# An elementwise add and GELU on one core: the first two loads of y cut 2 + 6 MB instead of 4 + 4, in one buffer, and the last wait moved from VectorE to ScalarE

## The chip, the cores and the metric

The kernel runs on one core of a Trainium2 chip. The time is that of one execution on the device, in microseconds (us). The profile shows one execution in detail; its times count from the first instruction's start. In it DVE is VectorE, ACT is ScalarE, POOL is GpSimd and SP is SyncE, the engine that issues all transfers here. TensorE computes nothing in this kernel, and the granted clock is 1.000 throughout.

## The reference

Two float32 arrays of 1024 x 4096 go in and one of the same shape comes out, 16.78 MB each:

```python
z = x + y
return (0.5 * z * (1 + np.tanh(np.sqrt(2 / np.pi) * (z + 0.044715 * z ** 3)))).astype(np.float32)
```

The kernel computes it as max(z, 0) + g(-|z|), where g is the tanh form of GELU. The two agree, since g(z) - g(-z) = z.

## The kernel before, in words

Each of the 128 partitions holds eight rows of the arrays, so 32768 columns in a row of 128 KB. The columns are worked in 16 chunks of 2048 (`CH`). A chunk c takes four steps:

- `add(c)`, L149: z = x + y, in place in the buffer that x was loaded into. VectorE does chunks 0, 2, 4, 6, 8 and 12, GpSimd the ten others.
- `mag(c)`, L154, and `gelu(c)`, L157: ScalarE takes |z| into a PSUM buffer and then the GELU of minus that, in place. There are two PSUM buffers (`PS = 2`), so `mag(c)` waits until `end(c - 2)` has read the buffer.
- `end(c)`, L166: VectorE forms max(z, 0) + w, in place in z. For chunk 8 (`FIRST`) it comes in two halves.

In the texts below add2 is `add(2)`, and so on. The whole of z, 128 KB in a partition, stays on the chip. y passes through two buffers of 8192 columns.

SP issues all nine transfers, in one queue, in this order: y0, x0, y1, x1, y2, y3, store 0, store 1, store 2 (L173, L174). The loads of x have 16384 columns each (8 MB), those of y 8192 (4 MB), the stores 16384, 10240 and 6144 (8, 5 and 3 MB). `begin_early` moves the first two ahead of the barrier at the start. y2 goes into the buffer of y0 and so waits on SP for add0 to add3; y3 waits for add4 to add7. Store 0 waits for end0 to end7 and, by a dependence that is put in by hand (L138), for the first half of end8. Store 1 waits for end12, store 2 for end15.

The order on each engine is written out by hand. GpSimd does its adds in rising order. ScalarE does mag0, gelu0, mag1, gelu1 and so on. VectorE's order comes from `by_dve`, which says ahead of which end each of its adds stands:

```python
    by_dve = {0: 0, 2: 0, 4: 2, 6: 4, 8: 8, 12: 10}
```

That gives add0, add2, end0, end1, add4, end2, end3, add6, end4, end5, end6, end7, add8, end8 (two halves), end9, add12, end10 to end15. An engine works its list in order, so an instruction that waits holds up those behind it.

At the end, `wait_late` takes the wait for the last store's landing out of SP's wait for everything. It is put at the very end of the program, as a wait of one engine that also sets the semaphore back.

Of the kernel before, what the change touches and what calls it, by code (L numbers as in the profile page):

```python
# [8 lines left out]
def begin_early(nc, count):  # L9


    head, body = (b.instructions for b in nc.main_func.blocks[:2])
    SP = mybir.EngineType.SP
    moved = [i for i in body if i.engine == SP and isinstance(i, mybir.InstDMACopy)][:count]
    assert not any(i.sync_info and i.sync_info.on_wait for i in moved)
    assert all(i.regs_accessed() == ((), ()) for i in moved)
    at = next(k for k, i in enumerate(head) if i.engine == SP)
    for k, i in enumerate(moved):
        body.remove(i)
        head.insert(at + k, i)  # L20


def wait_late(nc):

    body, end = (b.instructions for b in nc.main_func.blocks[1:3])
    last = [i for i in body if isinstance(i, mybir.InstDMACopy)][-1]
    (sem,) = [u.id for u in last.sync_info.on_update]
    all_done = end[0]  # L30
    reset = next(i for i in end if isinstance(i, mybir.InstDrain) and i.is_reset_sema)
    at = end.index(reset)
    clear = end[at + 1]
    first, stop = reset.reset_range_start, reset.reset_range_stop
    assert all_done.engine == mybir.EngineType.SP and reset.engine == mybir.EngineType.Pool
    assert isinstance(clear, mybir.InstISA) and clear.engine == mybir.EngineType.Pool
    waits = all_done.sync_info.on_wait
    (its,) = [w for w in waits if w.id == sem]

    end[0] = mybir.InstDrain(  # L40
        name=all_done.name, engine=all_done.engine, debug=all_done.debug, is_reset_sema=False,
        sync_info=mybir.SyncInfo(on_wait=[w for w in waits if w.id != sem], on_update=[]),
    )
    parts = []
    for f, e in ((first, sem), (sem + 1, stop)):
        if f < e:
            nc.gpsimd.sem_clear(range(f, e))
            parts.append(nc.cur_bb.bb.instructions.pop())
    end[at + 1 : at + 2] = parts
    end.append(  # L50
        mybir.InstEventSemaphore(
            name=clear.name, engine=mybir.EngineType.DVE, debug=clear.debug,
            sync_info=mybir.SyncInfo(
                on_wait=[its],
                on_update=[
                    mybir.SyncUpdate(
                        sync_type="semaphore", id=sem, ant_name=its.ant_name,
                        update_mode="sem-sub-imm", update_value=its.wait_value,
                    )
                ],  # L60
            ),
        )
    )


@with_exitstack
def kernel(
    ctx: ExitStack,
    tc: tile.TileContext,
    x: bass.AP,  # L70
    y: bass.AP,
    out: bass.AP,
):

    nc = tc.nc
    P = nc.NUM_PARTITIONS
    fp32 = mybir.dt.float32
    act = mybir.ActivationFunctionType
    alu = mybir.AluOpType

    N, D = x.shape
    assert N % P == 0
    TOT = N // P * D  # L90
    xv, yv, ov = (a.rearrange("(p n) d -> p (n d)", p=P) for a in (x, y, out))

    YS = 8192
    CH = 2048
    PS = 2
    xloads = [16384, 16384]
    yloads = [8192, 8192, 8192, 8192]
    FIRST = 8
    stores = [16384, 10240, 6144]

    def ranges(sizes):
        ends = [sum(sizes[: i + 1]) for i in range(len(sizes))]
        assert ends[-1] == TOT
        return [(e - f, e) for e, f in zip(ends, sizes)]

    xr, yr, sr, cr = (ranges(r) for r in (xloads, yloads, stores, [CH] * (TOT // CH)))
    C = len(cr)

    by_dve = {0: 0, 2: 0, 4: 2, 6: 4, 8: 8, 12: 10}

    def over(rs, lo, hi):
        return [i for i, (a, b) in enumerate(rs) if a < hi and b > lo]

    pool_sb = ctx.enter_context(tc.tile_pool(name="xz", bufs=1))
    pool_y = ctx.enter_context(tc.tile_pool(name="y", bufs=2))
    pool_w = ctx.enter_context(
        tc.tile_pool(name="w", bufs=PS, space=bass.MemoryType.PSUM)
    )

    zt = pool_sb.tile([P, TOT], fp32, tag="z", name="z")  # L120
    yt, wt, ends = {}, {}, {}

    def load_x(i):
        a, b = xr[i]
        nc.sync.dma_start(out=zt[:, a:b], in_=xv[:, a:b])

    def load_y(i):
        a, b = yr[i]
        s, o = divmod(a, YS)
        if o == 0:  # L130
            yt[s] = pool_y.tile([P, YS], fp32, tag="y", name=f"y{s}")
        nc.sync.dma_start(out=yt[s][:, o : o + b - a], in_=yv[:, a:b])  # L132

    def store(i):
        a, b = sr[i]
        ins = nc.sync.dma_start(out=ov[:, a:b], in_=zt[:, a:b])
        if i == 0:
            tc.add_manual_dep(  # L138
                ins.ins,
                ends[FIRST].name,  # L140
                mybir.DependencyInfo(mybir.DependencyClass.Sync, mybir.DependencyReason.DATA),
                reason="the stores join the queue when the last load is nearly done",
            )

    def add(c):
        a, b = cr[c]
        s, o = divmod(a, YS)
        eng = nc.vector if c in by_dve else nc.gpsimd
        eng.tensor_add(out=zt[:, a:b], in0=zt[:, a:b], in1=yt[s][:, o : o + b - a])  # L149

    def mag(c):
        a, b = cr[c]
        wt[c] = pool_w.tile([P, CH], fp32, tag="w", name=f"w{c}")
        nc.scalar.activation(out=wt[c], in_=zt[:, a:b], func=act.Abs)  # L154

    def gelu(c):
        nc.scalar.activation(  # L157
            out=wt[c], in_=wt[c], func=act.Gelu_apprx_tanh, scale=-1.0
        )

    def end(c):
        a, b = cr[c]
        parts = 2 if c == FIRST else 1
        n = (b - a) // parts
        for o in range(0, b - a, n):
            ins = nc.vector.scalar_tensor_tensor(  # L166
                out=zt[:, a + o : a + o + n], in0=zt[:, a + o : a + o + n], scalar=0.0,
                in1=wt[c][:, o : o + n], op0=alu.max, op1=alu.add,
            )
            ends.setdefault(c, ins.ins)  # L170


    sp = [(load_y, 0), (load_x, 0), (load_y, 1), (load_x, 1), (load_y, 2), (load_y, 3)]  # L173
    sp += [(store, i) for i in range(len(stores))]  # L174
    pool = [(add, c) for c in range(C) if c not in by_dve]
    dve, acts = [], []
    for c in range(C):
        dve += [(add, k) for k in sorted(by_dve) if by_dve[k] == c] + [(end, c)]
        acts += [(mag, c), (gelu, c)]

    needs = {
        load_x: lambda i: [],
        load_y: lambda i: [
            (add, c) for c in over(cr, yr[i][0] - 2 * YS, yr[i][1] - 2 * YS)
        ],
        add: lambda c: [(load_x, i) for i in over(xr, *cr[c])]
        + [(load_y, i) for i in over(yr, *cr[c])],
        mag: lambda c: [(add, c)] + ([(end, c - PS)] if c >= PS else []),
        gelu: lambda c: [(mag, c)],
        end: lambda c: [(gelu, c)],  # L190
        store: lambda i: [(end, c) for c in over(cr, *sr[i])] + [(end, FIRST)],
    }
    queues = [sp, pool, acts, dve]
    done = set()
    with tc.manual_schedule():
        one = pool_sb.tile([P, 1], fp32, tag="one", name="one")
        nc.vector.memset(one, 0.0)  # L197
        nc.scalar.activation(out=one, in_=one, func=act.Gelu_apprx_tanh)  # L198
        while any(queues):
            moved = False  # L200
            for q in queues:
                while q and all(n in done for n in needs[q[0][0]](q[0][1])):
                    fn, arg = q.pop(0)
                    fn(arg)
                    done.add((fn, arg))
                    moved = True
                    if q is not sp:
                        break
            assert moved, [q[:1] for q in queues]

    ctx.close()
    tc.close()
    tc.compile()  # L213
    begin_early(nc, 2)
    wait_late(nc)


# [28 lines left out]
```

## Time and profile before

| what | us |
|---|---|
| median of 3 runs | 120.11 (120.06 to 120.14) |
| the profiled execution | 120.11 |
| its span | 118.7 |
| VectorE busy, 24 instructions | 59.8 |
| ScalarE busy, 34 instructions | 60.8 |
| GpSimd busy, 14 instructions | 55.5 |
| one add on GpSimd, x10, mean | 5.56 |
| one add on VectorE, x6, mean | 4.01 |
| one mag and one gelu on ScalarE, x16, mean | 1.88 and 1.86 |
| one end on VectorE, x17, mean | 2.16 |

The table has the busy times of the page and the means of its groups by line. A mean mixes cases: an add of VectorE took between 2.28 and 6.59, one of GpSimd between 4.50 and 6.63. The nine transfers moved 50.33 MB in 1296 packets, at 424 GB/s over the span. In the slices each digit is the busy share of a fortieth of the span (2.97 us) in tenths. In lines of the timeline the first number is the start, the second the time, and the bracket tells how long the engine had been idle and what released it. The time of a transfer from issue to landing is in lines of its own, as least, median and greatest of a group.

### The profile page before, as it was taken

To read this page: it belongs to the slowest core of one execution; us is meant where nothing else is said; L and a number is where in the kernel's file an instruction comes from. 1 tells how busy PE (TensorE), PEld (TensorE's weight loads), DVE (VectorE), ACT (ScalarE), POOL (GpSimd) and SP (SyncE) were. 2 spreads that over 40 slices of the span, in tenths; PEclk is the share of its full clock that TensorE was granted. 3 is DMA by queue.
4 is the path that set the end of the run, shared out by engine and by line. 5 is a ranking of instruction groups with operands and counts; after the bars stand their busy time and mean duration, and the time that the engine had idled before them with its cause. 6 is when DMAs were issued, how large, how long until landed. Compare 5 with 4: busy or idle time off the path is not lost.

```text
span 118.7 us, 160 instructions
## 1 busy us (share of the span) xinstructions
DVE 59.8 (50%) x24; ACT 60.8 (51%) x34; POOL 55.5 (47%) x14
## 2 busy tenths in 40 slices
DVE  0000000000499999699994594257999457752000
ACT  5000000000067979999279705797798999940000
POOL 0000000000499999997000039999999999100000
DMA  7989888988899988988899898998899889999896
GB/s 232 475 364 696 353 353 353 707 353 353 353 409 475 530 353 353 707 353 353 353 475 409 387 497 353 519 541 353 353 486 574 353 353 442 442 442 442 373 422 265
DMA packets 1296, 50.33 MB, mean 424 GB/s; under 512 B 144, under 2 KB 144, under 8 KB 144
## 3 DMA queue, kind: packets, MB, share of 16 engines
q1 hardware_dynamic: 1296, 50.33, 98.7%
HBM read 33.55 MB, written 16.78 MB: 424 GB/s over the span
## 4 chain that ended last, share of the span: by engine, by line
DMA 47%; POOL 34%; POOLq 4%; ACT 3%; DVE 2%; issue 0%; SPq 0%; DVEq 0%
POOL z L149 34%; DMA z<-in_x_dram 26%; DMA y<-in_y_dram 21%; POOLq L213 4%; DVE z L166 2%; ACT w L154 2%; ACT w L157 2%; SPq L132 0%; POOLq L149 0%; DVEq L166 0%
## 5 line engine op out<-in xcount | busy, mean ns | idle before, releaser
L149 POOL TENSOR_TENSOR z<-z,y 128x2048 f32<-128x2048 f32 x10 | 55.3, 5561 | 45.5 <-DMA z<-in_x_dram 31.0
L154 ACT ACTIVATE w<-z 128x2048 f32<-128x2048 f32 x16 | 30.1, 1880 | 42.5 <-DVE z L149 36.0
L166 DVE SCALAR_TENSOR_TENSOR z<-z,w 128x2048 f32<-128x2048 f32 (+1 forms) x17 | 36.3, 2156 | 16.0 <-ACT w L157 16.0
L149 DVE TENSOR_TENSOR z<-z,y 128x2048 f32<-128x2048 f32 x6 | 24.0, 4012 | 30.3 <-DMA z<-in_x_dram 30.0
L157 ACT ACTIVATE w<-w 128x2048 f32<-128x2048 f32 x16 | 29.8, 1862 | 0.5
L198 ACT ACT_TABLE_LOAD x1 | 1.3, 1283 | 1.3 <-PEq L230 1.3
L197 DVE MEMSET one<- 128x1 f32 x1 | 0.1, 59 | 1.3 <-PEq L230 1.3
L198 ACT ACTIVATE one<-one 128x1 f32<-128x1 f32 x1 | 0.2, 203 | 0.0
L230 POOL MEMSET const-float32-0.0<- 128x1 f32 x1 | 0.1, 99 | 0.2 <-issue 0.2
L230 POOL MEMSET const-bfloat16-1.0<- 128x1 bf16 x1 | 0.1, 103 | 0.0
L230 POOL MEMSET const-uint8-127<- 128x1 uint8 x1 | 0.1, 102 | 0.0
L230 POOL MEMSET const-float32-1.0<- 128x1 f32 x1 | 0.1, 99 | 0.0
## 6 DMA issues: line engine op xcount, KB each, us to landing
y<-in_y_dram SPq DMA_DIRECT2D x4, 4096.0 KB, 23.7
out_dram<-z SPq DMA_DIRECT2D x1, 5120.0 KB, 15.1
out_dram<-z SPq DMA_DIRECT2D x1, 3072.0 KB, 11.1
z<-in_x_dram SPq DMA_DIRECT2D x2, 44.8
out_dram<-z SPq DMA_DIRECT2D x1, 21.7
```

Of the source, the lines that this page charges most:

```text
L149: eng.tensor_add(out=zt[:, a:b], in0=zt[:, a:b], in1=yt[s][:, o : o + b - a])
L154: nc.scalar.activation(out=wt[c], in_=zt[:, a:b], func=act.Abs)
L157: nc.scalar.activation(out=wt[c], in_=wt[c], func=act.Gelu_apprx_tanh, scale=-1.0)
L166: ins = nc.vector.scalar_tensor_tensor(out=zt[:, a + o : a + o + n], in0=zt[:, a + o : a + o + n], scalar=0.0, in1=wt[c][:, o : o + n], op ...
L197: nc.vector.memset(one, 0.0)
L198: nc.scalar.activation(out=one, in_=one, func=act.Gelu_apprx_tanh)
L213: tc.compile()
L230: nc = _bacc.Bacc("TRN2", target_bir_lowering=False, num_devices=1)
```

## The change

The first load of y takes 4096 columns, so rows of 16 KB, and the second 12288, rows of 48 KB. The third and the fourth stay at 8192. As a buffer of 8192 columns can't hold the second load, both buffers become one tile of 16384 columns, allocated once, in which a load finds its place by its columns modulo 16384. What y2 and y3 overwrite, and which adds they wait for, stays the same: y2 lands on columns 0 to 8191 of the tile and waits for add0 to add3, y3 on the rest and waits for add4 to add7. The order of instructions on every engine stays as it was. What changes is which load an add waits for: add0 and add1 wait for y0 and x0 as before, add2 and add3 now for y1, as add4 to add7 do. In `wait_late` the wait for the last store at the end goes to ScalarE.

```diff
-            name=clear.name, engine=mybir.EngineType.DVE, debug=clear.debug,
+            name=clear.name, engine=mybir.EngineType.Activation, debug=clear.debug,
...
-    YS = 8192
+    YS = 16384
...
-    yloads = [8192, 8192, 8192, 8192]
+    yloads = [4096, 12288, 8192, 8192]
...
-    pool_y = ctx.enter_context(tc.tile_pool(name="y", bufs=2))
...
-    yt, wt, ends = {}, {}, {}
+    yt = pool_sb.tile([P, YS], fp32, tag="y", name="y")
+    wt, ends = {}, {}
...
         a, b = yr[i]
-        s, o = divmod(a, YS)
-        if o == 0:
-            yt[s] = pool_y.tile([P, YS], fp32, tag="y", name=f"y{s}")
-        nc.sync.dma_start(out=yt[s][:, o : o + b - a], in_=yv[:, a:b])
+        o = a % YS
+        nc.sync.dma_start(out=yt[:, o : o + b - a], in_=yv[:, a:b])
...
         a, b = cr[c]
-        s, o = divmod(a, YS)
+        o = a % YS
         eng = nc.vector if c in by_dve else nc.gpsimd
-        eng.tensor_add(out=zt[:, a:b], in0=zt[:, a:b], in1=yt[s][:, o : o + b - a])
+        eng.tensor_add(out=zt[:, a:b], in0=zt[:, a:b], in1=yt[:, o : o + b - a])
...
-            (add, c) for c in over(cr, yr[i][0] - 2 * YS, yr[i][1] - 2 * YS)
+            (add, c) for c in over(cr, yr[i][0] - YS, yr[i][1] - YS)
```

## The prediction

> **What bounds the kernel now.** I read the page first: its table of queues says which resource has no room, and its slices say where each engine waits.
>
> ```profile
> span 118.7 us, 160 instructions
> ...
> DVE 59.8 (50%) x24; ACT 60.8 (51%) x34; POOL 55.5 (47%) x14
> ...
> DVE  0000000000499999699994594257999457752000
> ...
> POOL 0000000000499999997000039999999999100000
> DMA  7989888988899988988899898998899889999896
> ...
> q1 hardware_dynamic: 1296, 50.33, 98.7%
> ```
>
> All transfers go through one queue, and its packets take 98.7% of what the 16 transfer engines have in the span. No compute engine is over 51%. So the queue sets the time, and every microsecond in which it has nothing queued is added to the end. It can lose little more to the better: 1.3% of 118.7 is 1.5 us, and nearly all of that is the start (no byte in the first 1.0 us) and the landing of the last store.
>
> Second, where the next transfer of the queue comes from. These are the landings, from issue, of the y loads (L132), the x loads (L125) and the stores (L136), and then the stretch around the first store, in order of time:
>
> ```profile
> DMA to landing us min/median/max: 12.0/23.7/39.7
> ...
> DMA to landing us min/median/max: 30.9/44.8/58.7
> ...
> DMA to landing us min/median/max: 11.1/15.1/21.7
> ```
>
> ```profile
> 67.61 2.29 DVE L166 SCALAR_TENSOR_TENSOR z<-z,w 128x2048 f32<-128x2048 f32 x1 [1.47 <-ACT w L157]
> 70.18 2.29 DVE L149 TENSOR_TENSOR z<-z,y 128x2048 f32<-128x2048 f32 x1 [0.28 <-DMA y<-in_y_dram]
> 70.22 15.57 POOL L149 TENSOR_TENSOR z<-z,y 128x2048 f32<-128x2048 f32 x3 [14.56 <-DMA y<-in_y_dram]
> 72.50 1.88 ACT L154 ACTIVATE w<-z 128x2048 f32<-128x2048 f32 x1 [5.00 <-DVE z L149]
> 74.42 1.86 ACT L157 ACTIVATE w<-w 128x2048 f32<-128x2048 f32 x1
> 76.31 2.35 DVE L166 SCALAR_TENSOR_TENSOR z<-z,w 128x1024 f32<-128x1024 f32 x2 [3.84 <-ACT w L157]
> 77.56 0.35 SPq L136 DMA_DIRECT2D out_dram<-z  x1
> ```
>
> Landings before: y0 12.0; x0 31.29 (issued 0.43, 30.86 in the chain); y1 41.0 (1.26 + 39.7); x1 60.4; y2 70.08; y3 one y load of 4 MB later, 70.08 + 9.7 (41.0 - 31.3) = 79.8. Store 0 was issued at 77.56, only 2.3 us before that, and landed at 99.26. This is the thin place: VectorE had finished the last output of the first half (end7, 69.90) only 0.28 us before it began y2's first add, and with chunk 8 the path add, mag, gelu, half of end8 brought store 0 out just in time.
>
> Third, how VectorE's and GpSimd's adds stand beside each other:
>
> ```profile
> 31.39 2.29 DVE L149 TENSOR_TENSOR z<-z,y 128x2048 f32<-128x2048 f32 x1 [30.00 <-DMA z<-in_x_dram]
> 31.43 6.61 POOL L149 TENSOR_TENSOR z<-z,y 128x2048 f32<-128x2048 f32 x1 [30.99 <-DMA z<-in_x_dram]
> ...
> 33.60 6.59 DVE L149 TENSOR_TENSOR z<-z,y 128x2048 f32<-128x2048 f32 x1
> ...
> 51.16 4.50 POOL L149 TENSOR_TENSOR z<-z,y 128x2048 f32<-128x2048 f32 x1
> 52.19 5.62 DVE L149 TENSOR_TENSOR z<-z,y 128x2048 f32<-128x2048 f32 x1
> ```
>
> An add that starts first takes 2.29 on VectorE and 4.50 on GpSimd; one that starts while the other engine adds ends only its own 2.15 or 4.4 after the other has ended (38.04 + 2.15 = 40.19; 55.66 + 2.15 = 57.81; 33.68 + 4.36 = 38.04). They take turns, whole instructions at a time, and whoever is waiting is next. The STT of L166 reads PSUM and is not held up (2.27 to 2.29 throughout).
>
> **The change, part by part.** The profiled execution took 120.11, as the median of the runs; 1.44 of it lie outside the span of 118.67. The sums go against that one.
>
> *Sizes of y0 and y1.* The bytes stay: 2 + 6 MB instead of 4 + 4, 128 packets for each as before, so nine transfers and 1296 packets. y0 lands 4.85 earlier (half of 9.7), at 7.1, and x0 behind it at 26.4; y1 has all the same bytes ahead and lands at 41.0, x1 at 60.4. The price of packets of 16 and 48 KB is not in the trace; over 32 KB and 64 KB ones it is nearly one rate (9.7 us for 4 MB, 19.3 for 8 MB), so I take 0, between -0.1 and +0.1 for 256 of 1296 packets.
>
> *What moves with them.* Chunks 0 and 1 come 4.85 earlier: add0 at 26.5 to 28.8, GpSimd's add1 to 33.2, ScalarE's four to 37.0. But chunks 2 and 3 now need y1. VectorE's queue is add0, add2, end0, end1, add4: add2 ran from 33.60 and ended at 40.19; now it starts at 41.0 + 0.10 and ends at 43.4, with end0 and end1 stuck behind it and, through the two PSUM buffers, mag2 behind end0. The chain from there is the old one, with every datum there: end0 45.6, end1 47.8, GpSimd's add3 47.8 (43.4 + 4.4). So all of it shifts by 43.4 - 40.19 = 3.2 us, up to end7: 69.90 becomes 73.1. It cannot catch up: mag2 starts at 45.6, six chunks on ScalarE are 6 x 3.74 = 22.4, and the last end 2.3: 70.3 even with no wait in it.
>
> *The other queues that it passes.* SP issues y2 after add2 and add3 (44.62, now 47.8) and y3 after add6 and add7 (57.88, now 61.1). They must be queued 2.3 (below) ahead of the landings of x1, 60.4, and y2, 70.1: still 10 and 7 us of cover, cost 0; without it each late microsecond is one of the total. So y2 lands at 70.1 and y3 at 79.8.
>
> *What is late next.* At 70.1 VectorE still has end7 until 73.1, so GpSimd's add9, which used to come second, takes the turn: 70.22 to 74.72. VectorE's add8 is asked at 73.1 and ends at 74.72 + 2.15 = 76.87, where it was 72.47: 4.40 late. mag8, gelu8 and the first half of end8 follow as before, 5.09 later: store 0 is issued at 77.56 + 4.4 = 81.97, and the queue has run dry at 79.8.
>
> *The price.* A transfer into an idle queue is seen once: y0, issued at 0.00, landed at 12.0, of which 9.7 are data, so 2.3 us are lead. By that store 0 lands at 81.97 + 2.3 + 19.3 = 103.6 instead of 99.26: +4.3. Lower end: only the issue itself (0.35) and a landing as after the last store (0.3) count, 0.65: +2.7. The first read of y0 comes from HBM, a store reads SBUF, so I go a little below the row: +4.1. Stores 1 and 2: add12 is asked at 86.7, a microsecond after GpSimd began add13 (85.7 to 90.2), and ends at 92.4, where it was 87.94; end12 ends at 100.8 (96.27) and end15 at 111.8 (107.49). Store 1 is then issued 2.8 us before store 0's landing (it was 3.0), store 2 3.7 us before store 1's (3.8): no new gap, between 0 and +0.5 for the first, which has little to spare.
>
> *The wait at the end.* ScalarE instead of VectorE waits for the last store. Both queues are empty by then (ScalarE's last gelu ends 9 us ahead of it), nothing is queued behind it and no engine waits for it. VectorE's event began 0.03 after the landing at 118.62; ScalarE begins 0.04 after a release by GpSimd (81.31, 81.35). Cost 0, between -0.04 and +0.04.
>
> *Sum:* 120.11 + 4.1 = 124.2.
>
> One rule against the row: "DMA: Bandwidth & Descriptors", section Latency and other measured facts, gives about 0.6 us to the first byte of a transfer issued from this queue. This trace has 1.0 us without a byte at the start; by the page's figure the idle queue would cost 0.4 less and the time would be an estimated 123.8.
>
> **The rivals.**
> 1. *Not slower.* VectorE is ready at 70.2 all the same and add8 goes ahead of add9 as now; store 0 leaves at 77.56: 120.1. It needs 2.9 us out of the 29.7 from add2 to end7. For it: add6 waited 3.5 us for GpSimd's add7 (52.19 to 55.66), the largest slack in that stretch. Against: add6 stands behind end3, which shifts too, and GpSimd's queue shifts alike. Chance 4%.
> 2. *Half.* Add8 needn't wait for add9 to end: 73.1 + 2.3 = 75.4, store 0 at 80.5, +2.7: 122.8. Against it speak all three adds that VectorE began beside a running one. 5%.
> 3. *More.* Add12's wait for add13 or another lost turn makes store 1 late too. It decides once end12 ends after about 101.3; one more lost turn costs 4.5 less the slack of 0.5: 128. Or GpSimd also wins add3 before add2 at 41.1 and add8 slips behind add10: but by the same steps end7 would then be at 74.4, still under 74.72, and cost nothing. 7%.
>
> **How the numbers follow.** My forecast has 84%. Its own terms give 122.8 (lead of 0.65) to 124.9 (4.3 + 0.5), and the predicted time is 124.2; I widen to 122.7 to 125.3 for the terms of 0.1 and take in rival 2's edge. Outside lie rivals 1 and 3 and a few per cent of the rest. About 0.2% is what a measurement can tell from no change: faster by more 2%, same 3%, slower 95%.
>
> **What would show it.** In the changed kernel's trace: x0 lands near 26.4 and y1 at 41.0; add2 starts at 41.1; end7 ends near 73; add9 takes 4.5 and add8 ends near 76.9; store 0 is issued near 82 and the slices of DMA show a hole of 3 to 4 us between 79.5 and 83.5, no other one; stores 1 and 2 near 100.8 and 111.9. I am wrong if y2 or y3 is issued after its queue ran dry, if end7 is done by 70.2, or if the queue shows no hole.

## The result, and the profile after

The changed kernel takes 123.82 us (median of 6, 123.76 to 123.9) against 120.09 of the kernel before (median of 6): a ratio of 1.0306, interval 1.0293 to 1.0319. It is 3.7 us slower; 4.1 were forecast.

The page of the changed kernel has the same work in a longer span:

```profile
span 122.4 us, 161 instructions
...
DVE 57.8 (47%) x24; ACT 60.4 (49%) x34; POOL 55.5 (45%) x14
...
DMA  7999779859959897799789897709777979999596
...
q1 hardware_dynamic: 1296, 50.33, 95.8%
```

The same 1296 packets and 50.33 MB take 95.8% of the engines' time, where it was 98.7%. The missing part is one place: the only 0 among the slices is the 27th, from 79.6 to 82.6. No compute engine's busy time rose. The stretches of time around the hole show it sharper. Each line has the stretch and its length, the busy time of VectorE, ScalarE and GpSimd with the number of their instructions, the clock, the busy share of the transfer engines and the GB/s. (A packet counts in the stretch in which it starts, so a share can pass 1.)

```profile
76.00:79.50 3.50, 1.06 (x1) 2.37 (x2) 3.50 (x1) 1.00 0.70 300
79.50:83.00 3.50, 2.10 (x2) 3.47 (x3) 3.50 (x2) 1.00 0.04 19
83.00:86.00 3.00, 1.60 (x2) 3.00 (x2) 3.00 (x2) 1.00 1.58 677
```

The middle stretch in the kernel before:

```profile
79.50:83.00 3.50, 2.25 (x2) 2.80 (x2) 3.50 (x2) 1.00 0.82 356
```

For 3.5 us the queue of the changed kernel moves next to nothing. Why store 0 did not fill it is in the timeline of the changed kernel, from the place where y1 lands and from the one where y2 lands:

```profile
41.24 2.29 DVE L148 TENSOR_TENSOR z<-z,y 128x2048 f32<-128x2048 f32 x1 [12.16 <-DMA y<-in_y_dram]
...
45.77 1.88 ACT L153 ACTIVATE w<-z 128x2048 f32<-128x2048 f32 x1 [8.52 <-DVE z L165]
...
70.41 30.97 POOL L148 TENSOR_TENSOR z<-z,y 128x2048 f32<-128x2048 f32 x6 [11.42 <-DMA y<-in_y_dram]
70.92 2.29 DVE L165 SCALAR_TENSOR_TENSOR z<-z,w 128x2048 f32<-128x2048 f32 x1 [1.46 <-ACT w L156]
73.13 3.93 DVE L148 TENSOR_TENSOR z<-z,y 128x2048 f32<-128x2048 f32 x1
77.10 1.88 ACT L153 ACTIVATE w<-z 128x2048 f32<-128x2048 f32 x1 [6.27 <-DVE z L148]
79.01 1.86 ACT L156 ACTIVATE w<-w 128x2048 f32<-128x2048 f32 x1
...
80.90 2.35 DVE L165 SCALAR_TENSOR_TENSOR z<-z,w 128x1024 f32<-128x1024 f32 x2 [3.84 <-ACT w L156]
82.15 30.16 SPq L135 DMA_DIRECT2D out_dram<-z  x3
```

VectorE has waited 12.16 us for y1 when add2 begins at 41.24, and mag2 follows at 45.77. At 70.41 add9 begins on GpSimd, while VectorE still has end7 (70.92 to 73.21) to do. Add8 is asked at 73.13, starts working only when add9 has ended, and takes 3.93 instead of 2.29. From its end at 77.06 to store 0's issue the steps are the old ones, 5.09 us. So store 0 comes at 82.15 where it came at 77.56, and y3 had landed at 79.98.

The landings of the stores, from issue, close the account:

```profile
DMA to landing us min/median/max: 10.4/14.2/20.8
```

Store 0 lands 20.8 after its issue, at 102.92, which is 3.66 later than the 99.26 of before. Store 1 lands at 115.08 (3.73 later) and store 2 at 122.37 (3.75 later): the hole is carried to the end and less than 0.1 us is added to it.

### The profile page after: what moved, and what is told of

Its sections match the earlier page's. It is cut to its first block, busy times and chain, and to the rows that moved or that the text cites. A ratio compares the mean times of both kernels' runs of the same rounds, so it can differ in the third digit from the quotient of the medians.

```text
span 122.4 us, 161 instructions
## 1 busy us (share of the span) xinstructions
DVE 57.8 (47%) x24; ACT 60.4 (49%) x34; POOL 55.5 (45%) x14
## 2 busy tenths in 40 slices
DMA packets 1297, 50.33 MB, mean 411 GB/s; under 512 B 145, under 2 KB 145, under 8 KB 145
## 3 DMA queue, kind: packets, MB, share of 16 engines
q1 hardware_dynamic: 1296, 50.33, 95.8%
## 4 chain that ended last, share of the span: by engine, by line
DMA 33%; ACT 29%; DVE 15%; issue 14%; DVEq 0%
DMA y<-in_y_dram 33%; ACT w L153 18%; ACT w L156 10%; DVE z L165 8%; DVE z L148 7%; DVEq L165 0%
## 5 line engine op out<-in xcount | busy, mean ns | idle before, releaser
L148 DVE TENSOR_TENSOR z<-z,y 128x2048 f32<-128x2048 f32 x6 | 22.1, 3676 | 37.6 <-DMA z<-in_x_dram 25.4
## 6 DMA issues: line engine op xcount, KB each, us to landing
out_dram<-z SPq DMA_DIRECT2D x1, 20.8
```

The lines of the kernel that those rows point to most:

```text
L148: eng.tensor_add(out=zt[:, a:b], in0=zt[:, a:b], in1=yt[:, o : o + b - a])
```

## Experiments

The theory on trial is a chain: chunks 2 and 3 wait for the late y1, so add8 loses its turn to add9, so store 0 is issued too late, and the hole that this leaves in the queue is the price. The rivals: the sizes of the rows cost by themselves; the single buffer or the wait on ScalarE costs; the lateness of the whole chain counts and not the turn.

**Everything but the sizes.** In the changed kernel:

```diff
-    yloads = [4096, 12288, 8192, 8192]
+    yloads = [8192, 8192, 8192, 8192]
```

> The changed kernel with y loads of 4 + 4 MB again; the one buffer and ScalarE's wait at the end stay. Theory (the price is the late second load, through add8's lost turn and a late store 0): 120.1, within 0.1, with VectorE's add of chunk 8 ahead of GpSimd's at 70.2 and store 0 issued at 77.6. Rival (the buffer or the wait at the end costs): up to 123.8.

Measured: 120.14 against 120.01, ratio 1.001 (0.9992 to 1.0028). The buffer and the wait at the end cost nothing that this measurement can tell (at most 0.3%). In this profiled execution y2 landed at 70.78, 0.7 later than in the one of before, and store 0 was issued at 78.25; add8 was first again and the queue had no hole.

**One place in VectorE's order.** In the changed kernel, so with 2 + 6 MB:

```diff
-    by_dve = {0: 0, 2: 0, 4: 2, 6: 4, 8: 8, 12: 10}
+    by_dve = {0: 0, 2: 0, 4: 2, 6: 4, 8: 7, 12: 10}
```

> The changed kernel, with add8 ahead of end7 in VectorE's order and nothing else. Theory (lost turn): VectorE is idle when y2 lands and begins add8 at 70.4, a few hundredths ahead of GpSimd; it ends at 72.7, end7 at 74.9, gelu8 at 76.5; store 0 is issued at 77.8, before y3 lands at 80.0: no hole, 120.1, although y1 is as late and as large as in the changed kernel. Rival (packets of 16 and 48 KB, or the late chunks 2 to 7 as such): 123.8, or what is left of it.

Measured: 120.09 against 120.01, ratio 0.9998 (0.998 to 1.0016). The whole price is gone with the loads as they are, so packets of 16 and 48 KB cost nothing that shows (at most 0.2%), and chunks 2 to 7 may be late. The timeline where y2 lands:

```profile
70.35 2.29 DVE L148 TENSOR_TENSOR z<-z,y 128x2048 f32<-128x2048 f32 x1 [1.15 <-DMA y<-in_y_dram]
70.39 11.10 POOL L148 TENSOR_TENSOR z<-z,y 128x2048 f32<-128x2048 f32 x2 [11.66 <-DMA y<-in_y_dram]
72.56 2.28 DVE L165 SCALAR_TENSOR_TENSOR z<-z,w 128x2048 f32<-128x2048 f32 x1
72.67 1.88 ACT L153 ACTIVATE w<-z 128x2048 f32<-128x2048 f32 x1 [2.12 <-DVE z L148]
...
77.73 0.35 SPq L135 DMA_DIRECT2D out_dram<-z  x1
```

VectorE has put end7 off, is idle when y2 lands and begins 0.04 us ahead of GpSimd; add8 takes 2.29. End7 now ends at 74.84, later than in the changed kernel (73.21), and costs nothing: it runs while ScalarE works on chunk 8.

**The wait alone.** In the kernel before, with its own loads and buffers, add2 and add3 get a dependence on y1's load (`ydma` keeps the loads' instructions, `ins` is the add):

```diff
+        if c in (2, 3):
+            tc.add_manual_dep(
+                ins.ins,
+                ydma[1].ins.name,
...
-        add: lambda c: [(load_x, i) for i in over(xr, *cr[c])]
+        add: lambda c: [(load_x, i) for i in over(xr, *cr[c])] + [(load_y, 1)] * (c in (2, 3))
```

> The kernel before, with loads of 4 + 4 MB and two buffers, where add2 and add3 wait for y1's landing too. Theory: the same times as the changed kernel from 41 on, add8 ending at 77.0, store 0 issued at 82.1 and 123.8, with chunks 0 and 1 as late as in the kernel before (31.4), since they have cover. Rival (row sizes): 120.1.

Measured: 124.07 against 120.01, ratio 1.0324 (1.029 to 1.0358), which holds the changed kernel's 1.0306. The wait for y1 makes the price without any other part of the change:

```profile
31.50 2.29 DVE L150 TENSOR_TENSOR z<-z,y 128x2048 f32<-128x2048 f32 x1 [30.11 <-DMA z<-in_x_dram]
...
41.14 2.29 DVE L150 TENSOR_TENSOR z<-z,y 128x2048 f32<-128x2048 f32 x1 [7.35 <-DMA y<-in_y_dram]
...
73.04 3.93 DVE L150 TENSOR_TENSOR z<-z,y 128x2048 f32<-128x2048 f32 x1
...
82.06 0.35 SPq L137 DMA_DIRECT2D out_dram<-z  x1
```

Add0 is as late as in the kernel before, add2 as late as in the changed one, and from there the two agree within about 0.1 us. That chunks 0 and 1 come 4.7 earlier in the changed kernel is worth nothing.

**A smaller dose.** In the changed kernel, GpSimd adds chunk 8 and VectorE, in the same place, chunk 9:

```diff
-    by_dve = {0: 0, 2: 0, 4: 2, 6: 4, 8: 8, 12: 10}
+    by_dve = {0: 0, 2: 0, 4: 2, 6: 4, 9: 8, 12: 10}
```

> The changed kernel, where GpSimd adds chunk 8 and VectorE, in the same place of its order, chunk 9. Theory: GpSimd has chunk 8 ready at 70.4 + 4.5 = 74.9 in place of 77.0, so store 0 is issued at 80.05 in place of 82.15 and 2.1 us of the hole go: 121.7. If the time were set by VectorE's or ScalarE's whole work and not by the add of chunk 8, 123.8.

Measured: 121.72 against 120.01, ratio 1.0125 (1.0093 to 1.0157). VectorE is still the one that waits for its turn, but the chunk that waits is now 9, for which store 0 doesn't wait. Store 0 was issued at 80.62 and not at 80.05, since y2 landed 0.5 later in this execution than in the changed kernel's. y3 landed at 80.54, so store 0 came 0.08 us after it, where it was 2.17 in the changed kernel: the 2.1 us that were forecast.

**The second load cut in two.** In the changed kernel:

```diff
-    yloads = [4096, 12288, 8192, 8192]
+    yloads = [4096, 4096, 8192, 8192, 8192]
...
-    sp = [(load_y, 0), (load_x, 0), (load_y, 1), (load_x, 1), (load_y, 2), (load_y, 3)]
+    sp = [(load_y, 0), (load_x, 0), (load_y, 1), (load_y, 2), (load_x, 1), (load_y, 3), (load_y, 4)]
```

> The changed kernel with its second load of y cut in two, 2 + 4 MB, one behind the other ahead of x1. Theory: add2 and add3 have their data at 31.5 and no longer wait for 41; end7 is done before y2 lands, store 0 issued at 77.6, 120.1 (0 to 0.1 more for a tenth transfer). Rival (rows of 16 KB, or a small first load, cost by themselves): over 121.

Measured: 120.17 against 120.07, ratio 1.000 (0.9986 to 1.0015). With a load of 2 MB of their own, add2 and add3 have their data at 31.45, and VectorE is idle for 7.39 us before add8. This is the change's early start for chunks 0 to 3 without its price, and it gains nothing: the queue was full before and is full now.

**Only store 0 late.** In the kernel before:

```diff
-    FIRST = 8
+    FIRST = 9
```

> The kernel before, where the stores join the queue after the first half of end9 and not of end8. Its loads and adds are as before, but store 0 is issued at about 82.0, as in the changed kernel. Theory (the lateness of store 0 is the whole price): a hole as long as the changed kernel's less 0.15, and 123.6. If something else of the changed kernel costs, less; by the lead of 2.3 us that the start shows, 124.4.

Measured: 123.71 against 120.07, ratio 1.0293 (1.0272 to 1.0315). All adds stand as in the kernel before, and store 0 alone is late:

```profile
80.76 2.35 DVE L166 SCALAR_TENSOR_TENSOR z<-z,w 128x1024 f32<-128x1024 f32 x2 [2.14 <-ACT w L157]
...
82.01 0.35 SPq L136 DMA_DIRECT2D out_dram<-z  x1
```

Issued at 82.01 it costs 3.64 us; the changed kernel, with 82.15, costs 3.73. Store 0 landed 20.8 after its issue in this run, in the one with GpSimd's chunk 8, in the one with the wait alone and in the changed kernel. Its data take 19.35, as those of the loads of x do. Call the rest of the time from issue to landing the lead. For a store of 8 MB into an empty queue it is 20.8 - 19.35 = 1.4 us, and not the 2.3 of the first load.

**The lead of a load.** In the kernel before, y3 waits for end7 too:

```diff
+        if i == 3:
+            tc.add_manual_dep(
+                ins.ins,
+                ends[7].name,
...
-        ],
+        ] + [(end, 7)] * (i == 3),
```

> The kernel before, where y3 also waits for end7, so that SP issues it at 69.95 and the queue is empty when it comes. It measures the lead of a load into an empty queue within the run. If the lead is that of a store (landing 20.8 after issue, 19.35 of it data, so 1.4): y3 lands at 81.1 and the time is 121.3. If a load's lead is 2.3, as y0's at the start: 82.0 and 122.2.

Measured: 123.37 against 120.07, ratio 1.0267 (1.0242 to 1.0293). More than both expectations:

```profile
69.91 0.33 SPq L132 DMA_DIRECT2D y<-in_y_dram  x1
77.55 0.35 SPq L143 DMA_DIRECT2D out_dram<-z  x1
```

y3, issued at 69.91, landed at 83.38. Its data take 9.7, so 3.8 are lead. The packets of the trace, eight for each of the 16 transfer engines, say where they lie. The first packet of each engine starts 1.1 after the issue and takes 1.85 on average in place of 1.21; the next five are as ever; the last two, which start from 78.6 on, take 1.65 and 2.09. These two came after store 0 had been issued at 77.55.

**Load and store late.** The same with `FIRST = 9`, so that store 0 is issued when y3's packets are done:

> The kernel before, where y3 waits for end7 (issued at 69.91, into an empty queue) and store 0 for the first half of end9, so that it is issued near 82.0 and not at 77.55, when y3 was on its way. In the run with the late y3 alone the last two of each engine's eight packets of y3 took 1.65 and 2.09 us and not 1.21, and y3 landed at 83.38. If the store's issue in the middle of that load stretched them, y3 lands at 82.0 here (1.1 to the first packet, 0.64 in it, 9.7, 0.5). If the load had them long by itself, at 83.4 again. The time says little of it, since store 0 comes into an empty or nearly empty queue either way: 82.0 + 20.8 for store 0, then 19.4 and the rest outside the span, so 123.6.

Measured: 123.81 against 120.13, ratio 1.0300 (1.0272 to 1.0328). y3 was issued at 70.03 and landed at 82.15, a lead of 2.4, about that of the start, and its last packets took 1.21. Store 0, issued at 82.47, again landed 20.8 later. So the stretch goes with a store that is issued while this load is on its way. Why it does so for a load that came into an empty queue, and not in the kernel before, where store 0 is also issued while y3 is on its way, these runs don't say.

**A load late, but in time.** As the run with the late y3, but y3 waits for end6:

```diff
-                ends[7].name,
+                ends[6].name,
...
-        ] + [(end, 7)] * (i == 3),
+        ] + [(end, 6)] * (i == 3),
```

> The kernel before, where y3 waits for end6 and is issued at 66.2 and not at 57.88: late, but with 3.6 us of y2 ahead of it still. Theory (a load that is queued 2.3 us ahead has cover): no hole, 120.1. If a late load costs by itself, or its cover must be longer than 3.6 us, more, up to 123.4.

Measured: 120.5 against 120.13, ratio 1.002 (0.9998 to 1.0041). Issued at 66.16, 3.9 before y2 landed, y3 landed at 80.09, 0.2 later than in the kernel before, and its first packets took 1.36 on average instead of 1.21. There is no hole like those above; the profiled span is 118.8 against 118.7. A cost of up to 0.4% is not excluded.

**Three chunks in the first load.** In the changed kernel:

```diff
-    yloads = [4096, 12288, 8192, 8192]
+    yloads = [6144, 10240, 8192, 8192]
```

> The changed kernel with loads of y of 3 + 5 MB in place of 2 + 6, so that add2 has its data with x0 and only add3 waits for y1. Lost turn: end7 ends some 2 us sooner, near 71.1, but still after add9 began at 70.3; add9 goes first as in the changed kernel, add8 ends near 76.9 and the time is 123.8, as if nothing had been given back. If the time followed how late end7 is, 2 us of the 3.7 would be back: 121.8. If end7 ends before 70.3: 120.1.

Measured: 120.06 against 120.13, ratio 0.999 (0.9973 to 1.0007). The favoured expectation fell: end7 ended at 67.24, before y2's landing, and not near 71.1. It was the third case, end7 before 70.3. The timeline shows where the turns fell otherwise:

```profile
41.15 17.62 POOL L148 TENSOR_TENSOR z<-z,y 128x2048 f32<-128x2048 f32 x3 [5.44 <-DMA y<-in_y_dram]
...
42.17 5.62 DVE L148 TENSOR_TENSOR z<-z,y 128x2048 f32<-128x2048 f32 x1
...
52.11 2.28 DVE L148 TENSOR_TENSOR z<-z,y 128x2048 f32<-128x2048 f32 x1
...
64.95 2.29 DVE L165 SCALAR_TENSOR_TENSOR z<-z,w 128x2048 f32<-128x2048 f32 x1 [1.46 <-ACT w L156]
70.25 2.29 DVE L148 TENSOR_TENSOR z<-z,y 128x2048 f32<-128x2048 f32 x1 [3.02 <-DMA y<-in_y_dram]
```

GpSimd's add3 went first at 41.15 and VectorE's add4 waited for it. That put GpSimd's add5 behind add4, until 52.2, and VectorE asked for add6 at 52.11, just in time to go ahead of add7: 2.28 instead of 5.60. With mag2 begun at 40.08, before y1 landed, and no wait for add7, end7 came 6 us sooner than in the changed kernel. VectorE was busy with end1 until 42.24 and so couldn't take the turn at 41.15.

## Why the prediction was right

**The mechanism, in its order.** y1 landed at 41.22 (41.0 forecast), add2 began at 41.24 (41.1), end7 ended at 73.21 (73.1), add9 took its 4.5 first and add8 ended at 77.06 (76.87), store 0 was issued at 82.15 (81.97). Each is 0.1 to 0.2 late, as the landings of the loads are in this execution (y2 at 70.27, y3 at 79.98). The wait alone makes the same price (124.07), add8 put ahead of end7 takes all of it away (120.09), and a late store 0 without the rest makes it again (123.71). So the wait for y1, the turn that add8 lost through it and the late store are shown as the cause, and not only argued.

**The cover that was counted as cover.** y2 was issued at 47.96 and y3 at about 61.2, as forecast, with y1 of 6 MB and all its packets at the old rate; the queue has no other hole. Stores 1 and 2 added under 0.1 us: store 1 was issued at 100.86 and found store 0 still on its way. Its margin was 2.1 us and not 2.8, since store 0 landed at 102.92 and not at 103.6.

**The size: one term was off.** The price was put at 4.1 from a lead of 2.3 us seen at the start, taken down a little. The term that was mis-sized is this lead: for a store of 8 MB it is 1.4 in all five runs that show it. The issue came 0.18 later than forecast, which gave some of the error back. Worked with what was measured, store 0 lands 82.15 + 20.77 - 99.26 = 3.66 later, and the last store 3.75. The prediction went below the row since the first read comes from HBM and a store reads SBUF. The runs do show a load paying more at its first packet (1.85 instead of 1.21 in the run with the late y3; for store 0 of the changed kernel 2.46 instead of 2.42), but not that HBM is the reason. The lead of 0.65 at the lower end was too small by about as much as 2.3 was too large.

The lead also says how much room store 0 had before. It was issued 2.3 us ahead of y3's landing and needs 1.4 of them, so only 0.9 were free. It came 82.15 - 77.56 = 4.59 later, and 4.59 - 0.9 is the price of 3.7.

**The rule on the first byte.** The Trainium skill's page "DMA: Bandwidth & Descriptors", section Latency and other measured facts, has about 0.6 us to the first byte of a transfer from this queue. Here store 0's packets started 0.84 after the start of the issue at the earliest (80.62 to 81.46, in the run with GpSimd's chunk 8), and loads' about 1.0; the measurement decides. That the time by the page's figure, 123.8, was met is chance: it replaced one term and kept the start's other ones.

**The rivals.** *Not slower* fell for this kernel, but what it needed can happen: with 3 + 5 MB add6 goes ahead of add7, end7 is done at 67.2 and the time is 120.06. The wait for add7 was thus the right place to look, though in that run add2 no longer waits for y1 either. *Half*, add8 beside add9, did not occur in any run. *More* did not either: add12 waited for add13 as worked out (86.86 to 92.51), and store 1 still came in time.

**The wait at the end.** ScalarE's event began 0.02 after the last landing, VectorE's 0.03; the run with the old sizes tells no difference in the time. ScalarE's last gelu ended 12.8 us ahead of that landing (109.57, 122.37); the prediction's 9 was too small, and nothing hung on it.

## What to carry to other kernels

Where one transfer queue is full from start to end, only the moments at which its next transfer might be late matter: list each transfer's issue beside the end of the one ahead of it, take off the lead, and find the smallest margin (here store 0, 2.3 us ahead and 0.9 to spare). A change anywhere upstream is free until it eats that margin; from there on each late microsecond is one of the total. The lateness itself can come in steps, since one lost turn between two engines cost a whole add of the other (4.5 us). Before loads are re-cut, see which instruction is first in line for the late part and what stands behind it in the same queue; an early start elsewhere does not pay for it.

## What the runs showed that I had not expected

- The lead into an empty queue is not one number: 1.4 us from issue to landing beyond the data for a store of 8 MB, in the changed kernel and four more runs, and 2.3 to 2.4 for a load of 4 MB, at the start and in the middle of the kernel. First loads of 2 and 3 MB had 2.2 to 2.5 as well. No run has a load and a store of one size into an empty queue, so the runs don't show that the direction alone makes the difference.
- A load that came into an empty queue had its last packets stretched from 1.21 to 1.65 and 2.09 us when a store was issued behind it, which cost a further 1.4 us; with the store issued later it was gone. The cause is open.
- VectorE's and GpSimd's adds took turns, in every place looked at, in the order in which they were asked, to a few hundredths: 0.04 us decided who was first when both waited for the same landing, and in the run with 3 + 5 MB, where GpSimd had the turn at 41.15, end7 was done at 67.24 where 71.1 had been expected.
